# Scores of both maps in couples, with 64-row matmuls for the queries' low halves, in an encoder layer on Trainium2

## The chip, the cores and the metric

The kernel runs on one core of one Trainium2 chip. The metric is the device time of one execution in microseconds (us); of several runs the median is given. A profile is one execution taken by the hardware profiler; its span runs from the first instruction to the last. Engines are named as in the profile: PE is TensorE (PEld its weight loads), DVE is VectorE, ACT is ScalarE, POOL is GpSimd, SP is SyncE, which here issues nearly all DMAs (its queue is SPq). Each engine works through its own queue in order, and waits at an instruction until what it needs has been signalled.

## The reference, cut to what matters

One encoder layer with a convolution branch and a differential-attention branch is applied to two groups of rows, of 2048 and of 1024 positions, with the same weights. The change concerns the attention alone:

```python
def diff_attention(q, k, v, lam):            # 4 heads, head width 64, two maps c per head, values 128 wide
    def block(q_blk):                        # 128 queries
        s = jnp.einsum('bqhcd,bkhcd->bhcqk', q_blk, k).astype(jnp.float32) * scale
        p = jax.nn.softmax(s, axis=-1)
        a = p[:, :, 0] - lam * p[:, :, 1]
        return jnp.einsum('bhqk,bkhe->bqhe', a.astype(v.dtype), v)
```

Everything is float32. Before it come the input projections, the convolution and the rotary embedding; after it a normalisation per head, gates, two output projections and a LayerNorm.

## The kernel before

Matrices are split into a high half (rounded for TensorE) and a low half (the rest), and products are summed from halves, so that TensorE's fast float32 mode gives float32 accuracy.

There are three stages, one behind the other. The first computes all input projections, the convolution and the rotary embedding, and writes queries, keys, values and gates to DRAM, queries and keys each as a high and a low half (`qd`, `kd`). The second is the attention. The third merges the branches and projects.

**Attention.** The work is cut into `pairs`: one head of one group (`h`, `g`) and 256 queries, that is two blocks `j` of 128 queries. There are 32 pairs with 2048 keys (the long group) and then 16 with 1024 keys (the short group). A head's keys lie in tiles `km[c, hf]`, for map `c` and 1024 keys `hf`: the upper 64 rows hold the high half, the lower 64 the low half. A pair's queries lie in four tiles, for each map one with the high half and one with the low half, each twice, above and below (L135 to L143). A product over 128 rows with the high tile so gives high x high + high x low, and one with the low tile low x high + low x low.

The engines' order is written out by a loop that counts steps in `now` (L907). In a step it emits, in this order:

- `score` (L808): for one block, one map and 1024 keys, four matmuls of 512 columns (two column halves, two query halves) into a PSUM tile `s` of two banks, of which there are two. VectorE evicts it (L820) into `e`, scaled and with a running minimum. `e` is a tile of 2048 columns in SBUF; there are `NE` = 8 places, and a new row of scores waits in the loop while they are taken.
- `turn` (L842): four transposes of 128 x 128 on TensorE for two key tiles of a pair that is old enough; ScalarE takes the high half `ah` from PSUM. A long pair has 8 turns, a short one 4. The first stands `LAGS` = 8 steps behind the pair's last score.
- what is due in the middle (`mid`): `soften` (L824), the exponential of one row of `e` on ScalarE with its sum, one step behind the row's last score; the squares of a finished pair.
- `product` (L857): six matmuls with the values, for the turn two steps earlier; then VectorE takes the low half `al` of this step's turn (L852).
- what is due late (`late`): `combine` (L834), two steps behind the score of map 1: VectorE inverts the sum, GpSimd forms the factor `cc`, multiplies map 1's exponentials by it and adds them to map 0's, over the whole row. A pair's turns read that sum for both of its blocks.

Every fourth step also splits a piece of the third stage's weights, while there are any (`resident`, L886): a DMA of 128 KB into one buffer, and four steps later ScalarE's high and GpSimd's low half. When the last long pair is done, `factors` (L746) computes the long group's normalisation factors on VectorE in one go.

SyncE's DMAs are not in the written order; a scheduler places them. In the attention they are a pair's queries (L141, eight of 64 KB), the heads' keys and values, the weight pieces, and small stores. The first pair's queries go through ScalarE's queue at the end of the first stage, in which PSUM is divided among `px` (two buffers), `py`, `pv`, `pz` and others (L163 and L164). The attention's PSUM tiles take over those banks in the order in which the pools are made (L804 to L806).

## Time and profile before

| | us |
|---|---|
| median of 3 runs | 2705.11 (2703.72 to 2706.64) |
| the profiled execution | 2712.73 |
| its span | 2710.9 |

Busy time of each engine in that span, and its instructions, from the head of the profile:

```profile
PE 2592.6 (96%) x12546; PEld 2108.6 (78%) x12546; DVE 2096.7 (77%) x2766; ACT 1195.8 (44%) x1957; POOL 1439.1 (53%) x957
```

and the busy tenths of the same span in 40 equal slices of 67.8 us, where 9 is 90% or more:

```profile
PE   6999899999999999999996999999999999999998
POOL 3577644235431213443545999888889633343343
```

The attention takes the slices in which GpSimd stands at 8 and 9. In answers of the trace a row of the timeline has its start in us, its duration in us, engine, line, operation, what it writes and reads, and in brackets the idle time ahead of it with what ended that. Rows of a group have count, busy time in us, mean ns of one, and the idle time ahead. Rows by stretches of the span have for each engine the busy time and the count, then TensorE's granted clock, the DMA share and GB/s. Matmuls overlap in the pipe, so their durations add up to more than the time between their starts.

### The profile page before, as it was taken

How to read it: one execution, taken by the hardware profiler on the slowest of the kernel's cores; microseconds unless marked ns; L12 is line 12 of the kernel's file. 1: busy time of each engine (PE TensorE's matmuls, PEld its weight loads, DVE VectorE, ACT ScalarE, POOL GpSimd, SP SyncE). 2: the span in 40 equal slices, each digit the busy share in tenths (PEclk: the TensorE clock that was granted, in tenths of full speed). 3: DMA queues.
4: the chain of work that ended last, by engine and by line, in shares of the span. 5: the costliest groups of instructions: out<-in, count | busy, mean ns of one | idle time of the engine just before them, and what ended most of it. 6: DMA issues, size and time to landing. Idle time of an engine off the chain costs nothing. (4 is left out here: it accounts for less than half of the span.)

```text
span 2710.9 us, 37888 instructions
## 1 busy us (share of the span) xinstructions
PE 2592.6 (96%) x12546; PEld 2108.6 (78%) x12546; DVE 2096.7 (77%) x2766; ACT 1195.8 (44%) x1957; POOL 1439.1 (53%) x957
## 2 busy tenths in 40 slices
PE   6999899999999999999996999999999999999998
PEld 3877688787778877778874888888888777777877
DVE  6699888779888358997656888888888776667765
ACT  4323333522232333442435888877789622222221
POOL 3577644235431213443545999888889633343343
PEclk6999999999999999999998999999999999999999
DMA  5578876868986775776976141413153476656553
GB/s 184 198 251 304 273 235 234 300 204 292 316 289 223 244 266 185 244 255 198 300 230 175 57 118 55 108 40 102 40 132 94 156 240 190 195 182 225 171 172 104
DMA packets 339572, 527.15 MB, mean 194 GB/s; under 512 B 42176, under 2 KB 126640, under 8 KB 339376
## 3 DMA queue, kind: packets, MB, share of 16 engines
q1 hardware_dynamic: 338736, 524.20, 59.8%
q8 instruction: 100, 1.64, 0.3%
q14 instruction: 96, 0.79, 0.1%
q10 hardware_dynamic: 640, 0.52, 0.1%
HBM read 344.00 MB, written 167.99 MB: 189 GB/s over the span
## 5 line engine op out<-in xcount | busy, mean ns | idle before, releaser
L229 POOL TENSOR_TENSOR wl<-wq,wh 128x512 fp32r<-128x512 f32 x198 | 267.7, 1355 | 591.5 <-ACT wh L228 511.7
L335 DVE SCALAR_TENSOR_TENSOR acc<-uc,conv_dw,acc 128x1024 f32<-128x1024 f32 (+1 forms) x348 | 444.3, 1277 | 4.1
L818 PE MATMUL s<-km,qq 128*128 128x512 f32 x1280 | 355.2, 400 | 24.9 <-DVE e L820 20.2
L840 POOL TENSOR_TENSOR e<-e 128x2048 f32<-128x2048 f32 (+1 forms) x96 | 373.1, 3886 | 8.0
L831 ACT ACTIVATE e<-e,mx 128x2048 f32<-128x2048 f32 (+1 forms) x192 | 329.3, 1715 | 3.1 <-DVE e L820 3.1
L818 PEld LDWEIGHTS s<-km,qq 128*128 128x128 f32 x1280 | 222.2, 191 | 62.1 <-DVE e L820 26.3
L854 DVE TENSOR_TENSOR al<-tp,ah 128x512 fp32r<-128x512 f32 x320 | 220.3, 689 | 55.7 <-ACT ah L849 55.5
L584 PE MATMUL pv<-xh,wh 128*128 128x512 f32 x528 | 219.0, 415 | 35.5 <-DVE ta L598 25.1
L820 DVE TENSOR_SCALAR_CACHE_REDUCE e<-s 128x1024 f32<-128x1024 f32 x192 | 233.5, 1216 | 16.6 <-PE s L818 15.8
L849 ACT ACTIVATE ah<-tp 128x512 fp32r<-128x512 f32 x320 | 189.4, 593 | 99.3 <-PE tp L847 97.3
L584 PE MATMUL px<-xh,wh 128*128 128x512 f32 x528 | 212.0, 401 | 8.5 <-ACT xh L275 5.3
L584 PE MATMUL pv<-xh,wl 128*128 128x512 f32 x528 | 215.7, 409 | 0.2
L584 PE MATMUL pv<-xl,wh 128*128 128x512 f32 x528 | 215.7, 409 | 0.0
L584 PE MATMUL px<-xh,wl 128*128 128x512 f32 x528 | 211.6, 401 | 4.2 <-POOL wl L229 4.2
L584 PE MATMUL pz<-xh,wh 128*128 128x512 f32 x528 | 211.3, 400 | 3.3 <-ACT xh L275 1.5
L584 PE MATMUL pz<-xh,wl 128*128 128x512 f32 x528 | 211.0, 400 | 0.4 <-DMA wl<-wsd_3l 0.2
L584 PE MATMUL px<-xl,wh 128*128 128x512 f32 x528 | 210.7, 399 | 0.0
L584 PE MATMUL pz<-xl,wh 128*128 128x512 f32 x528 | 210.0, 398 | 0.2 <-DVE xl L276 0.2
L99 PE MATMUL ops<-ah,vv 128*128 128x256 f32 x640 | 207.3, 324 | 0.2 <-ACT row L880 0.2
L94 POOL TENSOR_TENSOR zl<-zraw,zh 128x512 fp32r<-128x512 f32 x88 | 123.5, 1406 | 157.8 <-ACT zh L93 133.0
L847 PE MATMUL tp<-ident,e 128*128 128x128 f32 x1280 | 192.7, 273 | 1.5 <-DVE al L854 1.2
L847 PEld LDWEIGHTS tp<-ident,e 128*128 128x128 f32 x1280 | 158.4, 141 | 45.3 <-DVE al L854 3.7
(228 smaller groups left out, 6334.9 us busy)
## 6 DMA issues: line engine op xcount, KB each, us to landing
wq<-in_w_in SPq DMA_DIRECT2D x220, 256.0 KB
qq<-qd SPq DMA_DIRECT2D x376, 64.0 KB
zraw<-in_w_out SPq DMA_DIRECT2D x88, 256.0 KB
ev<-ev SPq DMA_DIRECT2D x192, 64.0 KB
kd<-ev SPq DMA_DIRECT2D x48, 256.0 KB
qd<-ev SPq DMA_DIRECT2D x48, 256.0 KB
vd<-ev SPq DMA_DIRECT2D x48, 256.0 KB
mcd<-ev SPq DMA_DIRECT2D x48, 256.0 KB
```

The lines of the kernel that those rows point to most:

```text
L94: (lo_engine or nc.vector).tensor_sub(lo, src, hi.bitcast(F32))
L99: nc.tensor.matmul(ps, ah, bh, start=first, stop=False)
L229: (lo_engine or (nc.vector if i in summed and si else nc.gpsimd)).tensor_sub(lo, src, hi.bitcast(F32))
L335: nc.vector.scalar_tensor_tensor(dst, src, dw_sb[:, c, k:k + 1], acc, op0=ALU.mult, op1=ALU.add)
L584: nc.tensor.matmul(ps, w[a][:, k], X[o, k][x], start=fresh and k == a == x == 0, stop=k == 3 and x == 1, skip_group_check=not fresh)
L818: nc.tensor.matmul(s[:, n * 512:(n + 1) * 512], p.qt[2 * c + i][:, j * P:(j + 1) * P], p.km[c, hf][:, n * 512:(n + 1) * 512], start=i == 0 ...
L820: nc.vector.tensor_scalar(p.e[j, c][:, hf * 1024:(hf + 1) * 1024], s, -SCALE, mx[:, hf - 1:hf] if hf else None, op0=ALU.mult, op1=ALU.min, ...
L831: nc.scalar.activation(e, e, AF.Exp, bias=p.mx[j, c][:, nh - 1:nh], scale=-1.0, accum_out=sc)
L840: nc.gpsimd.tensor_add(e0, e0, e)
L847: nc.tensor.transpose(tp[:, i, j * P:(j + 1) * P], p.e[j, 0][:, kt * P:(kt + 1) * P], ident)
L849: nc.scalar.activation(ah, tp, AF.Copy)
L854: nc.vector.tensor_sub(al, tp, ah.bitcast(F32))
```

## The change

- **Couples.** `score` now computes both maps of a block for 1024 keys at once, in every second step (`now % 2`). For each map two matmuls of 128 rows with the high queries come first; then, alternating between the maps, four matmuls of 64 rows multiply the low queries by the high keys alone (low x low is left out). For that, a tile `ql` holds the low queries of map 0 in the upper and of map 1 in the lower 64 rows, and map 1's keys are loaded with the halves exchanged. A pair has five DMAs for its queries instead of eight. Both evictions follow.
- **Times in the loop.** The exponential of map 0 stands one step behind the couple, that of map 1 two, the combination four. `LAGS` is 9, and `OPENING` sets 5 and 7 for the first two pairs. `NE` is 10.
- **First pair.** Its combination is done on VectorE, in two operations, without GpSimd.
- **PSUM.** `pv` and `pz` get a pool of their own, made first, and the attention's pools are made in the order `ops`, `tp`, `s`, so that `s` gets the banks of `py` and of the convolution's tiles.
- **Factors.** For the long group they are computed in four parts, spread over steps.

```diff
 KAPPA = 2.0 ** -11
-LAGS = (8, 8)
-NE = 8
+LAGS = (9, 9)
+OPENING = (5, 7)
+NE = 10
 NST = NH * sum(LENS) // P
...
                 for i in range(2):
-                    nc.sync.dma_start(kk.bitcast(F32)[i * HD:(i + 1) * HD],
+                    o = (i ^ c) * HD
+                    nc.sync.dma_start(kk.bitcast(F32)[o:o + HD],
                                       kd[self.g][self.h][i, c * HD:(c + 1) * HD, hf * 1024:(hf + 1) * 1024])
...
             self.steps, self.lag = self.L // 256, LAGS[g]
+            self.first = g == h == qp == 0
             self.at, self.e, self.mx, self.qt = 10 ** 6, {}, {}, []
             self.col = col0[g][h] + 2 * qp
 
         def load(self, head, maps=(0, 1), queue=nc.sync):
             self.km, self.vv = head.km, head.vv
+            q = slice(self.qp * 256, self.qp * 256 + 256)
             for c in maps:
-                for i in range(2):
-                    qq = kvp[0].tile([P, 256], F32R, name=f"qq{c}{i}", bufs=2)
-                    for r in range(2):
-                        queue.dma_start(qq.bitcast(F32)[r * HD:(r + 1) * HD, :],
-                                          qd[self.g][self.h][i, c * HD:(c + 1) * HD, self.qp * 256:self.qp * 256 + 256])
-                    self.qt.append(qq)
+                qq = kvp[0].tile([P, 256], F32R, name=f"qq{c}", bufs=2)
+                for r in range(2):
+                    queue.dma_start(qq.bitcast(F32)[r * HD:(r + 1) * HD, :], qd[self.g][self.h][0, c * HD:(c + 1) * HD, q])
+                self.qt.append(qq)
+            if maps[-1]:
+                self.ql = kvp[0].tile([P, 256], F32R, name="ql", bufs=2)
+                queue.dma_start(self.ql.bitcast(F32), qd[self.g][self.h][1, :, q])
 
     pairs = [Pair(g, h, qp) for g in range(2) for h in range(NH) for qp in range(LENS[g] // 256)]
+    for p, p.lag in zip(pairs, OPENING):
+        pass
 
...
                       for n, b in (("a_s", 6), ("a_n", 5), ("a_u", 2)))
+
+        psL = pool(name="a_pl", bufs=1, space=PSUM)
         psX = pool(name="a_px", bufs=2, space=PSUM)
...
             px = psX.tile([P, 512], F32, name="px")
-            py, pv, pz = (psP.tile([P, 512], F32, name=n) for n in ("py", "pv", "pz"))
+            py, pv, pz = (x.tile([P, 512], F32, name=n) for x, n in ((psP, "py"), (psL, "pv"), (psL, "pz")))
             t_ = {}
...
         nc.vector.reciprocal(s1, ps[:n, :P])
+        yield
         for _ in range(2):
             nc.vector.scalar_tensor_tensor(s0, s1, 1.0 / KAPPA, s0, op0=ALU.mult, op1=ALU.mult)
         nc.vector.tensor_scalar(f, s0, 1.0 / P, epsl[:n], op0=ALU.mult, op1=ALU.add)
+        yield
         nc.vector.reciprocal(f, f)
+        yield
         nc.vector.tensor_scalar(s0, s0, thr[:n], lscale[:n], op0=ALU.is_le, op1=ALU.mult)
         nc.vector.tensor_mul(s1, s1, s0)
         nc.scalar.activation(f, f, AF.Sqrt)
         nc.vector.tensor_mul(f, f, s1)
         nc.sync.dma_start(rrd[g].rearrange("h (t q) -> (h t) q", q=P), f)
+        yield
 
...
         ep = pool(name="b_e", bufs=NE)
+        psO = pool(name="b_o", bufs=2, space=PSUM)
+        psT = pool(name="b_t", bufs=2, space=PSUM)
         psS = pool(name="b_s", bufs=2, space=PSUM)
-        psT = pool(name="b_t", bufs=2, space=PSUM)
-        psO = pool(name="b_o", bufs=2, space=PSUM)
-
-        def score(p, j, c, hf):
-            if hf == 0:
-                if c == 0 or p.L == 2048:
-                    p.tile = ep.tile([P, 2048], F32, name="e")
-                p.e[j, c] = p.tile[:, c * p.L % 2048:][:, :p.L]
-                p.mx[j, c] = sm.tile([P, 2], F32, name="mx")
-            mx = p.mx[j, c]
-            s = psS.tile([P, 1024], F32, name="s")
-            for n in range(2):
-                for i in range(2):
-                    nc.tensor.matmul(s[:, n * 512:(n + 1) * 512], p.qt[2 * c + i][:, j * P:(j + 1) * P],
-                                     p.km[c, hf][:, n * 512:(n + 1) * 512], start=i == 0, stop=i == 1)
-            nc.vector.tensor_scalar(p.e[j, c][:, hf * 1024:(hf + 1) * 1024], s, -SCALE,
-                                    mx[:, hf - 1:hf] if hf else None, op0=ALU.mult, op1=ALU.min,
-                                    accum_out=mx[:, hf:hf + 1])
+
+        def score(p, j, hf):
+
+
+            q, ns, ss = slice(j * P, (j + 1) * P), [slice(n * 512, (n + 1) * 512) for n in range(2)], []
+            for c in range(2):
+                if hf == 0:
+                    if c == 0 or p.L == 2048:
+                        p.tile = ep.tile([P, 2048], F32, name="e")
+                    p.e[j, c] = p.tile[:, c * p.L % 2048:][:, :p.L]
+                    p.mx[j, c] = sm.tile([P, 2], F32, name="mx")
+                ss.append(psS.tile([P, 1024], F32, name="s"))
+                for n in ns:
+                    nc.tensor.matmul(ss[c][:, n], p.qt[c][:, q], p.km[c, hf][:, n], start=True, stop=False)
+            for n in ns:
+                for c in range(2):
+                    r = slice(c * HD, (c + 1) * HD)
+                    nc.tensor.matmul(ss[c][:, n], p.ql[r, q], p.km[c, hf][r, n], start=False, stop=True)
+            for c in range(2):
+                mx = p.mx[j, c]
+                nc.vector.tensor_scalar(p.e[j, c][:, hf * 1024:(hf + 1) * 1024], ss[c], -SCALE,
+                                        mx[:, hf - 1:hf] if hf else None, op0=ALU.mult, op1=ALU.min,
+                                        accum_out=mx[:, hf:hf + 1])
 
...
             nc.vector.reciprocal(cc, sc)
+            if p.first:
+                nc.vector.scalar_tensor_tensor(cc, cc, neglam, stats[:, p.col + j:p.col + j + 1], op0=ALU.mult, op1=ALU.mult)
+                nc.vector.scalar_tensor_tensor(e0, e, cc, e0, op0=ALU.mult, op1=ALU.add)
+                return
             nc.gpsimd.tensor_mul(cc, cc, stats[:, p.col + j:p.col + j + 1])
...
             if p is pairs[NH * LENS[0] // 256 - 1]:
-                late[now + 4].append(lambda: factors(0, sm, psT.tile([P, 512], F32, name="tp")))
+                def f():
+                    steps = factors(0, sm, psT.tile([P, 512], F32, name="tp"))
+                    next(steps)
+                    for i in range(3):
+                        late[now + 1 + i].append(lambda: next(steps))
+                late[now + 4].append(f)
 
...
         for p in pairs:
-            todo += [(p, j, c, hf) for j in range(2) for c in range(2) for hf in range(p.L // 1024)]
+            todo += [(p, j, hf) for j in range(2) for hf in range(p.L // 1024)]
             ready += [(p, i) for i in range(p.steps)]
...
                     f()
-                if todo and (todo[0][3] or live[0] < NE):
-                    p, j, c, hf = todo.pop(0)
-                    live[0] += hf == 0 and (c == 0 or p.L == 2048)
-                    if (j, c, hf) == (0, 0, 0):
+                if todo and now % 2 and (todo[0][2] or live[0] + todo[0][0].L // 1024 <= NE):
+                    p, j, hf = todo.pop(0)
+                    live[0] += 0 if hf else p.L // 1024
+                    if (j, hf) == (0, 0):
                         nxt = pairs.index(p) + 1
...
                                 x.load(kv[x.g, x.h])
-                    score(p, j, c, hf)
-                    if (j, c, hf) == (1, 1, p.L // 1024 - 1):
-                        p.at = now + p.lag
+                    score(p, j, hf)
                     if hf == p.L // 1024 - 1:
-                        def f(p=p, j=j, c=c, now=now):
-                            sc = soften(p, j, c)
-                            if c == 1:
+                        if j:
+                            p.at = now + p.lag
+
+                        def f(p=p, j=j, now=now):
+                            soften(p, j, 0)
+
+                            def f():
+                                sc = soften(p, j, 1)
+
                                 def f():
                                     combine(p, j, sc)
                                     live[0] -= p.L == 2048
-                                late[now + 2].append(f)
+                                late[now + 4].append(f)
+                            mid[now + 2].append(f)
                         mid[now + 1].append(f)
...
             if R is rows[0]:
-                factors(1, io, psY.tile([P, 512], F32, name="y"))
+                for _ in factors(1, io, psY.tile([P, 512], F32, name="y")):
+                    pass
             steps = {kind: [lambda i=i: next(i)] * (CT + 2) if nxt else [] for kind in "uo"
                      for i in [nxt and prepare(nxt, kind)]}
             both = lambda *fs: lambda: [f() for f in fs]

```

**VectorE, in the long group.** Here `e,mx<-s` is an eviction of the first 1024 keys, `e,mx<-s,mx` that of the second, `al` a turn's low half, and the reciprocal the start of a combination. Before:

```order
L820 TENSOR_SCALAR e,mx<-s 128x1024
L854 TENSOR_TENSOR al<-tp,ah 128x512
L820 TENSOR_SCALAR e,mx<-s,mx 128x1024
L854 TENSOR_TENSOR al<-tp,ah 128x512
L837 RECIPROCAL cc<-ssum 128x1
L820 TENSOR_SCALAR e,mx<-s 128x1024
```

and in the changed kernel:

```order
L840 TENSOR_SCALAR e,mx<-s 128x1024 x2
L878 TENSOR_TENSOR al<-tp,ah 128x512 x2
L840 TENSOR_SCALAR e,mx<-s,mx 128x1024 x2
L878 TENSOR_TENSOR al<-tp,ah 128x512
L857 RECIPROCAL cc<-ssum 128x1
L878 TENSOR_TENSOR al<-tp,ah 128x512
```

The evictions of the two maps now stand together, and the reciprocal stands behind both and a low half; that of a pair's second block is in the step that is five ahead of the pair's first turn, where it was six ahead.

**TensorE, in the long group,** one step before (`s` scores, `tp` a turn, `ops` a product):

```order
L818 MATMUL s<-km,qq_14031 128x512
L818 MATMUL s<-km,qq_14034 128x512
L818 MATMUL s<-km,qq_14031 128x512
L818 MATMUL s<-km,qq_14034 128x512
L847 MATMUL tp<-ident,e 128x128 x4
L99 MATMUL ops<-ah,vv 128x256
L100 MATMUL ops<-ah,vv 128x256
L101 MATMUL ops<-al,vv 128x256
L99 MATMUL ops<-ah,vv 128x256
L100 MATMUL ops<-ah,vv 128x256
L101 MATMUL ops<-al,vv 128x256
```

and an odd step of the changed kernel, with the turn that opens the next:

```order
L833 MATMUL s<-km,qq_13318 128x512 x2
L833 MATMUL s<-km,qq_13321 128x512 x2
L837 MATMUL s<-km,ql 128x512 x4
L871 MATMUL tp<-ident,e 128x128 x4
L100 MATMUL ops<-ah,vv 128x256
L101 MATMUL ops<-ah,vv 128x256
L102 MATMUL ops<-al,vv 128x256
L100 MATMUL ops<-ah,vv 128x256
L101 MATMUL ops<-ah,vv 128x256
L102 MATMUL ops<-al,vv 128x256
L871 MATMUL tp<-ident,e 128x128 x4
```

A step of the first kind has four score matmuls, a turn and a product; in the changed kernel eight score matmuls stand ahead of two turns with their products.

## The prediction

> **What bounds the kernel now.** I read the page's busy shares first, then the busy time by stretches of the span, then the timeline engine by engine, and last the groups by line and shape inside the attention stage. The page gives TensorE 96% of the span, but that is an average over three stages. The change touches the second alone, from about 1420 to 2150 us. Busy time there, by engine (PE, PEld, DVE, ACT, POOL):
>
> ```profile
> 1420.00:1440.00 20.00, 13.67 (x46) 8.58 (x45) 12.91 (x21) 9.19 (x11) 1.30 (x1) 0.91 0.92 256
> 1440.00:1460.00 20.00, 9.88 (x31) 6.24 (x31) 9.55 (x17) 7.18 (x9) 11.47 (x7) 0.79 0.93 255
> 1500.00:1600.00 100.00, 100.00 (x677) 88.83 (x675) 88.66 (x155) 84.00 (x130) 92.52 (x55) 1.00 0.28 77
> 1800.00:1900.00 100.00, 100.00 (x677) 88.92 (x676) 88.66 (x155) 79.64 (x118) 85.50 (x42) 1.00 0.30 83
> 2080.00:2100.00 20.00, 20.00 (x139) 17.78 (x138) 17.34 (x32) 18.80 (x41) 19.15 (x17) 1.00 0.30 80
> ```
>
> There is an opening with idle engines up to 1475, then the long group (32 pairs of query blocks, 2048 keys), where TensorE never idles and VectorE and GpSimd are at 86 to 93%, and then the short group (16 pairs, 1024 keys), where GpSimd is at 96%. So whatever TensorE saves in the long group can be used only until the next engine, or the next chain of waits, is reached. One step of the long group on TensorE:
>
> ```profile
> 1526.73 1.09 PE L818 MATMUL s<-km,qq 128*128 128x512 f32 x4
> 1527.66 0.60 PE L847 MATMUL tp<-ident,e 128*128 128x128 f32 x4
> 1528.02 0.37 PE L99 MATMUL ops<-ah,vv 128*128 128x256 f32 x1
> 1528.22 0.28 PE L100 MATMUL ops<-ah,vv 128*128 128x256 f32 x1
> ...
> 1528.82 1.09 PE L818 MATMUL s<-km,qq 128*128 128x512 f32 x4
> ```
>
> From start to start, four score matmuls take 0.93 us (0.2325 each), a turn (four transposes) 0.36, a product 0.80: 2.09 us a step. A pair is eight steps. Counted in the timeline, the first turn of the fourth pair and that of the last long pair are
>
> ```profile
> 1521.40 0.60 PE L847 MATMUL tp<-ident,e 128*128 128x128 f32 x4
> 1994.60 0.60 PE L847 MATMUL tp<-ident,e 128*128 128x128 f32 x4
> ```
>
> and (1994.60 - 1521.40)/28 = **16.90 us a pair**.
>
> **The couple on TensorE.** It replaces eight matmuls of 128 rows (1.86 us) by four of 128 rows and four of 64. No row shows a 64-row matmul. If the halves of the two maps run side by side, they take 0.465 us, a couple 1.40; one after another it is 1.86 as before. I take 1.40, since the two halves use different rows of the array and different PSUM tiles; the other end is a rival. Each couple also enters and leaves 64-row work. The nearest row for such a passage is the first product after a turn: 0.20 us to its neighbour (1528.02 to 1528.22) where others of its kind are 0.12 apart (0.80 us hold six), so 0.08 to 0.09. For the upper end:
>
> ```profile
> L818 PE MATMUL s<-km,qq 128*128 128x512 f32 x1280 | 355.2, 400 | 24.9 <-DVE e L820 20.2
> ```
> ```profile
> 1423.17 0.50 PE L584 MATMUL pz<-xh,wl 128*128 128x512 f32 x1 [0.16 <-DMA wl<-wsd_3l]
> 1423.51 0.39 PE L584 MATMUL pz<-xl,wh 128*128 128x512 f32 x1
> ```
>
> A matmul of 512 columns lasts 0.40 us against 0.2325 from start to start, so waiting for an empty pipe costs 0.17; one whose weights came late held the next back by 0.34 - 0.23, 0.10 more: 0.27. I take s = 0.09, between 0 and 0.27. TensorE alone would need 4 x (1.40 + 2.32 + 0.18) + 0.23 for the sums = 15.8 us a pair, 1.1 less than now.
>
> The Trainium skill ("TensorEngine Tiling (Array Packing)", Key Properties) says that a change of tiling mode drains TensorE, which speaks against this change. Its page "TensorE: Matmul & The Clock Gate" (Single matmul latency) has (398 + N)/2.4 ns for one warm matmul, 379 ns at N = 512, against 216 back to back; the trace has 400 and 233. An estimate of s from these two pages would be 0.16, and the loop below would come to 17.8 us.
>
> **The chain that takes over.** The change also moves the combination of a map pair. Before, it stood six steps ahead of the pair's first turn, now five, and VectorE meanwhile evicts both maps ahead of the reciprocal. What each link costs, on VectorE and GpSimd:
>
> ```profile
> 1863.10 0.69 DVE L854 TENSOR_TENSOR al<-tp,ah 128x512 fp32r<-128x512 f32 x1
> 1863.78 1.28 DVE L820 TENSOR_SCALAR_CACHE_REDUCE e<-s,mx 128x1024 f32<-128x1024 f32 x1
> 1864.98 0.08 DVE L820 DVE_READ_ACCUMULATOR e<-s,mx 128x1 f32 x1
> 1865.23 0.69 DVE L854 TENSOR_TENSOR al<-tp,ah 128x512 fp32r<-128x512 f32 x1 [0.16 <-ACT ah L849]
> 1865.84 0.15 DVE L837 RECIPROCAL cc<-ssum 128x1 f32<-128x1 f32 x1
> ...
> 1866.13 0.19 POOL L838 TENSOR_TENSOR cc<-cc,stats 128x1 f32<-128x1 f32 x1 [0.15 <-DVE cc L837]
> 1866.43 2.06 POOL L839 TENSOR_SCALAR e<-e,cc,neglam 128x2048 f32<-128x2048 f32 x1
> 1868.58 4.63 POOL L840 TENSOR_TENSOR e<-e 128x2048 f32<-128x2048 f32 x1
> ```
>
> An eviction takes 1.20 us until the next can start, the low half `al` 0.61, and from the reciprocal to the end of GpSimd's addition it is 1873.21 - 1865.84 = 7.37. The addition that releases a turn, and the turn that waited for it in the opening, are
>
> ```profile
> 1458.33 4.55 POOL L840 TENSOR_TENSOR e<-e 128x2048 f32<-128x2048 f32 x1
> ...
> 1463.19 0.60 PE L847 MATMUL tp<-ident,e 128*128 128x128 f32 x4
> ```
>
> 0.31 us from its end. An eviction starts some 0.20 after the turn behind its scores does. So from the end of a couple's scores to the first turn that the combination behind them releases: 0.20 + 2 x 1.20 + 0.61 + 7.37 + 0.31 = **10.9 us**. In that time TensorE has five turns, five products and two couples to do, 5 x 1.16 + 2 x (1.40 + 2s) = 8.6 + 4s, about 9.0. Nothing else can be done meanwhile, since TensorE's queue is in order: the turn blocks the products and the next couple behind it, for about 1.9 us in each pair. (Before, the chain is one eviction shorter, 9.7 us, and has six whole steps, 12.5 us, to lie beside.)
>
> The loop closes over one pair: 10.9, then turn and product 1.16, a couple 1.40, two turns and products 2.32, a couple 1.40: 17.17 + 4s = **17.5 us** a pair with s = 0.09 (17.2 with none, 18.2 with 0.27). ScalarE's two exponentials, now in neighbouring steps, could hold a low half back by up to 0.3; I cost that at nothing, the wait for GpSimd hides most of it. So the long group loses 0.6 us in each of 28 pairs: **+17 us** (+8 to +37). VectorE's own work, two evictions and two low halves, 2 x 1.20 + 2 x 0.61 = 3.6 us a couple, 14.5 a pair, lies below that, and so does GpSimd's:
>
> ```profile
> 1603.85 0.74 POOL L894 TENSOR_TENSOR w_attn_ol<-wraw,w_attn_oh 128x256 fp32r<-128x256 f32 x1
> ...
> 1865.24 0.74 POOL L94 TENSOR_TENSOR sql<-sq,sqh 128x256 fp32r<-128x256 f32 x1
> ```
>
> two combinations of 7.08 (1866.13 to 1873.21), a square's low half and, while they last, two weight pieces, 16.4 at most.
>
> **The opening.** PSUM's new order lets the first scores start before the last projections are evicted. But the first eviction of scores stands on VectorE behind those same evictions and gains nothing there. What holds the opening are ScalarE's pieces of resident weights, which wait for a small transfer and hold the exponentials behind them:
>
> ```profile
> 1448.48 5.37 SPq L141 DMA_DIRECT2D qq<-qd  x8
> ...
> 1453.22 0.42 ACT L893 ACTIVATE w_conv_projh<-wraw 128x256 fp32r<-128x256 f32 x1 [9.95 <-DMA qq<-qd]
> ...
> 1467.04 0.42 ACT L893 ACTIVATE w_conv_projh<-wraw 128x256 fp32r<-128x256 f32 x1 [9.43 <-DMA wraw<-in_w_conv_proj]
> ```
>
> These stand in the changed kernel at the same places. SyncE's issues fall from eight to five a pair, at 5.37/8 = 0.67 us, so these pieces come 2 and up to 4 us sooner. For VectorE's combination of the first pair the nearest row has half its columns:
>
> ```profile
> L1026 DVE SCALAR_TENSOR_TENSOR xr<-xr,mv,ln_g_b 128x1024 f32<-128x1024 f32 x24 | 36.4, 1515 | 0.1
> ```
>
> so it takes about 3 us for GpSimd's 7.4, and the first turn may come at 1457 instead of 1463. Then the second and third pair, with short lags, run into the same 10.9 us chain with nothing to fill it. I put the first turn of the fourth pair at 1524, **+2 us**, between -8 and +8: the gain of some 6 us is spent there. The loads themselves lie under the long group otherwise (DMA share 0.28), as does the space for ten exponentials; both cost nothing.
>
> **The short group.** GpSimd sets its pace, back to back:
>
> ```profile
> 2112.41 0.19 POOL L838 TENSOR_TENSOR cc<-cc,stats 128x1 f32<-128x1 f32 x1
> 2121.02 0.18 POOL L838 TENSOR_TENSOR cc<-cc,stats 128x1 f32<-128x1 f32 x1
> L838 POOL TENSOR_TENSOR cc<-cc,stats 128x1 f32<-128x1 f32 x32 | 6.7, 209 | 9.3 <-DVE cc L837 6.4 <-ACT ah L849 2.9
> ```
>
> 8.6 us a pair, which the couple doesn't touch (TensorE would need 8.0). GpSimd's idle 9.3 us should go: 6.4 where no place for exponentials was free, 2.9 behind the unsplit factors on VectorE. But its first short combination now waits for the last long one, about 3 us. **-6 us**, between -10 and 0. The third stage is not touched.
>
> **Sum.** +2 + 17 - 6 = +13 us on the profiled execution (2712.73 us, span 2710.9; 7.6 above the median of the three runs). Taken to the median: 2705.1 + 13 = 2718 us.
>
> **Rivals.**
> *The gain stays* (not slower). If the result of GpSimd is there when its turn comes, which needs 1.9 us less in the chain or as much more work ahead of the turn, a pair is bound by GpSimd at 16.4 us in the 11 pairs that still carry weight pieces and by TensorE at 15.8 in the other 17: 11 x -0.5 + 17 x -1.1 = -24, with -3 in the opening and -6 in the short group 2672 us. For it speaks that no engine's sum forbids it; against it each link of the chain.
> *The halves do not overlap.* Then a couple is 1.86 + 2s, the loop 17.5 + 0.93 = 18.4: +42, and the short group is bound by TensorE at 8.95 us (+5): 2705 + 2 + 42 + 5 - 6 = 2748 us. The Trainium skill speaks against it ("TensorE: Matmul & The Clock Gate", Part 3): matmuls in different row groups run concurrently. No row here shows it.
> *A wash.* The wait on GpSimd comes, but the passages cost nothing (+8), the opening keeps its 6 us and the short group gives 6 or more: 2705 us, within 4.
>
> **How the numbers follow.** Chances: the forecast 0.47 (2711 to 2740), the gain 0.27, the wash 0.16, the serial halves 0.10. A difference under 0.2%, 5.4 us, cannot be told from no change. Faster 0.27, same 0.16, slower 0.57. The range goes from 2670, past the middle of the gain, to 2746, just short of the serial halves; below and above it I leave about 0.18. The forecast's own range is 2711 to 2740.
>
> **What would show it.** Right: in the long group the first turn of each pair waits for GpSimd's addition 1.5 to 2.5 us, 17.3 to 17.8 us from pair to pair, and TensorE is busy about nine tenths; four 64-row matmuls take about 0.5 us from start to start. Wrong: no wait for GpSimd at the turns and 16 us a pair (the gain), or couples of 1.9 us and more (serial halves). In the short group GpSimd should have no idle stretch of several microseconds.

## The result, and the profile after

The changed kernel takes **2746.69 us** (median of 4 runs, 2742.96 to 2749.87), the kernel before in the same session 2704.41 (4 runs, 2702.43 to 2706.64): a ratio of **1.0153, 95% interval 1.0138 to 1.0167**, 42 us slower. The prediction had the sign and less than a third of the size: 13 us, with a range that ended at 2746, 0.7 us short of the median. The profiled execution of after took 2749.87 us, its span is 2747.7. That of before lay 8.3 us over its median, this one 3.2 over its own, so the spans differ by 36.8 us where the medians differ by 42.3.

Busy time by stretches of after (PE, PEld, DVE, ACT, POOL, then the granted clock), for the same stretches as before:

```profile
1420.00:1440.00 20.00, 12.41 (x34) 5.80 (x32) 9.15 (x16) 6.64 (x7) 0.00 (x0) 0.67 1.04 290
1440.00:1460.00 20.00, 11.21 (x26) 4.89 (x27) 14.68 (x22) 4.67 (x7) 0.73 (x1) 0.50 0.95 223
1500.00:1600.00 100.00, 91.66 (x611) 69.30 (x610) 81.19 (x144) 76.82 (x118) 87.83 (x51) 1.00 0.25 66
1800.00:1900.00 100.00, 94.21 (x647) 73.37 (x645) 83.29 (x148) 77.91 (x116) 81.83 (x39) 1.00 0.23 61
2080.00:2100.00 20.00, 19.16 (x135) 15.07 (x136) 17.04 (x32) 18.43 (x39) 19.06 (x19) 1.00 0.43 114
```

In the long group TensorE now idles for 6 to 8% and issues 611 and 647 matmuls in 100 us where it issued 677; VectorE and GpSimd have become less busy too. That is a chain, not an engine at its limit. The page's groups name where the idle time lies:

```profile
L840 DVE TENSOR_SCALAR_CACHE_REDUCE e<-s 128x1024 f32<-128x1024 f32 x192 | 227.3, 1222 | 52.9 <-PE s L837 52.7
L871 PE MATMUL tp<-ident,e 128*128 128x128 f32 x1280 | 210.6, 284 | 48.0 <-POOL e L864 31.5
```

and the same two groups on the page of before:

```profile
L820 DVE TENSOR_SCALAR_CACHE_REDUCE e<-s 128x1024 f32<-128x1024 f32 x192 | 233.5, 1216 | 16.6 <-PE s L818 15.8
L847 PE MATMUL tp<-ident,e 128*128 128x128 f32 x1280 | 192.7, 273 | 1.5 <-DVE al L854 1.2
```

The turns on TensorE waited 1.5 us in all before, most of it for VectorE; they wait 48.0 now, 31.5 of it for GpSimd's addition.

To see in which stretch the time lies I read marks from TensorE's timeline of each kernel: the end of the first stage's last projection matmul (P), the start of a pair's first turn (its second transposition where that one had to wait for the combination, otherwise its first; T0, T3, T16, T31 for long pairs, numbered from 0, and T47 for the last short one), the start of the last turn and the end of the span. In us; the long group also per pair:

| kernel | P to T0 | T0 to T3 | a pair, T3 to T16 | a pair, T16 to T31 | T31 to T47 | T47 to last turn | last turn to end |
|---|---|---|---|---|---|---|---|
| before | 37.2 | 58.2 | 16.90 | 16.90 | 146.1 | 4.9 | 565.2 |
| **after** | 37.5 | 67.5 | 17.86 | 17.60 | 146.7 | 7.2 | 570.4 |
| e1, lags of ten | 37.2 | 69.6 | 18.23 | 16.84 | 151.4 | 8.9 | 567.9 |
| e4, before with PSUM order | 36.9 | 57.8 | 16.91 | 16.90 | 145.0 | 5.3 | 577.7 |
| e5, e1 and pieces moved | 37.0 | 68.8 | 16.86 | 16.84 | 149.8 | 7.6 | 573.5 |
| e6, halves in one row group | 40.0 | 69.4 | 18.52 | 18.43 | 158.2 | 6.9 | 571.0 |
| e7, PSUM order undone | 37.5 | 67.7 | 17.82 | 17.61 | 146.8 | 7.2 | 560.3 |
| e8, nine for pairs 0 and 1 | 41.8 | 55.7 | 17.89 | 17.61 | 148.0 | 6.0 | 571.2 |
| e9, e5, e7 and e8 together | 41.8 | 56.4 | 16.85 | 16.83 | 150.9 | 8.8 | 562.3 |
| e10, e9 with spread exponentials | 41.5 | 53.5 | 16.40 | 16.40 | 151.8 | 9.0 | 561.5 |
| e12, before with ten places | 37.4 | 57.7 | 16.90 | 16.90 | 143.1 | 4.6 | 563.5 |
| e13, after with spread alone | 38.2 | 65.1 | 17.27 | 17.32 | 146.8 | 7.4 | 578.8 |

After against before: opening +9.6, long group 13 x 0.96 + 15 x 0.70 = +23, short group +0.6, tail +2.3, third stage +5.2; P itself came 3.7 us sooner (1422.3 against 1426.0; it lay at 1420.4 and 1421.5 in e4 and e12, which share that stage with before, so the profiled run of before was late there by chance). The sum is 37, the difference of the spans. The last column also scatters between profiles of kernels that are alike there: over all runs it lies between 560.3 and 565.2 us with the PSUM order of before, and between 567.9 and 578.8 with that of after.

One pair of the long group, TensorE and then the engines it waits for:

```profile
1799.77 1.08 PE L833 MATMUL s<-km,qq 128*128 128x512 f32 x4
1800.78 0.73 PE L837 MATMUL s<-km,ql 64*128 64x512 f32 x4
1801.44 0.65 PE L871 MATMUL tp<-ident,e 128*128 128x128 f32 x4
1801.85 0.36 PE L100 MATMUL ops<-ah,vv 128*128 128x256 f32 x1
...
1809.77 0.66 PE L871 MATMUL tp<-ident,e 128*128 128x128 f32 x4
...
1810.98 0.27 PE L871 MATMUL tp<-ident,e 128*128 128x128 f32 x1
1812.25 0.55 PE L871 MATMUL tp<-ident,e 128*128 128x128 f32 x3 [1.00 <-POOL e L864]
```
```profile
1801.26 0.69 DVE L878 TENSOR_TENSOR al<-tp,ah 128x512 fp32r<-128x512 f32 x1 [0.67 <-ACT ah L873]
1801.87 1.27 DVE L840 TENSOR_SCALAR_CACHE_REDUCE e<-s,mx 128x1024 f32<-128x1024 f32 x1
...
1804.88 0.15 DVE L857 RECIPROCAL cc<-ssum 128x1 f32<-128x1 f32 x1
...
1809.98 0.69 DVE L878 TENSOR_TENSOR al<-tp,ah 128x512 fp32r<-128x512 f32 x1 [1.17 <-ACT ah L873]
```
```profile
1805.18 0.19 POOL L862 TENSOR_TENSOR cc<-cc,stats 128x1 f32<-128x1 f32 x1 [1.90 <-DVE cc L857]
1805.47 2.06 POOL L863 TENSOR_SCALAR e<-e,cc,neglam 128x2048 f32<-128x2048 f32 x1
1807.61 4.59 POOL L864 TENSOR_TENSOR e<-e 128x2048 f32<-128x2048 f32 x1
```

These rows show the chain of the prediction, link by link: the couple's scores end at 1801.44, two evictions and a low half later stands the reciprocal (1804.88), and 7.37 us after that TensorE goes on with the turn (1812.25): 10.81 us, where 10.9 was forecast. The first part is 3.44 us instead of 3.21 and the second 7.37 instead of 7.68, so that two small errors cancel. The turn's first transposition needs only the first query block, which was combined earlier; the other three wait. A couple takes 1.68 us (1799.77 to 1801.44).

### The profile page after: what moved, and what is told of

It is laid out like the page before. It is cut to its first block, busy times and chain, and to the rows that moved or that the text cites. A ratio compares the mean times of both kernels' runs of the same rounds, so it can differ in the third digit from the quotient of the medians.

```text
span 2747.7 us, 37631 instructions
## 1 busy us (share of the span) xinstructions
PE 2592.6 (94%) x12546; PEld 2032.8 (74%) x12546; DVE 2091.8 (76%) x2770; ACT 1199.7 (44%) x1957; POOL 1422.9 (52%) x951
## 5 line engine op out<-in xcount | busy, mean ns | idle before, releaser
L864 POOL TENSOR_TENSOR e<-e 128x2048 f32<-128x2048 f32 (+1 forms) x94 | 362.5, 3856 | 7.8
L840 DVE TENSOR_SCALAR_CACHE_REDUCE e<-s 128x1024 f32<-128x1024 f32 x192 | 227.3, 1222 | 52.9 <-PE s L837 52.7
L871 PE MATMUL tp<-ident,e 128*128 128x128 f32 x1280 | 210.6, 284 | 48.0 <-POOL e L864 31.5
L871 PEld LDWEIGHTS tp<-ident,e 128*128 128x128 f32 x1280 | 141.9, 141 | 115.9 <-issue 39.5
L833 PE MATMUL s<-km,qq 128*128 128x512 f32 x640 | 186.9, 410 | 15.4 <-DVE e L840 10.5
L237 ACT ACTIVATE wh<-wq 128x512 fp32r<-128x512 f32 x198 | 122.9, 622 | 148.4 <-PE pv L593 116.0
```

The source lines that it names most:

```text
L833: nc.tensor.matmul(ss[c][:, n], p.qt[c][:, q], p.km[c, hf][:, n], start=True, stop=False)
L840: nc.vector.tensor_scalar(p.e[j, c][:, hf * 1024:(hf + 1) * 1024], ss[c], -SCALE, mx[:, hf - 1:hf] if hf else None, op0=ALU.mult, op1=ALU.min,
L864: nc.gpsimd.tensor_add(e0, e0, e)
L871: nc.tensor.transpose(tp[:, i, j * P:(j + 1) * P], p.e[j, 0][:, kt * P:(kt + 1) * P], ident)
```

## The experiments

Each ratio is to the kernel before, with its 95% interval; between kernels I use the stretch that was edited.

**e1, lags of ten steps.** From the changed kernel:

```diff
-LAGS = (9, 9)
+LAGS = (10, 10)
```

> The changed kernel with lags of ten steps instead of nine (the opening's two short lags stay). Theory 1 (GpSimd's result comes too late for the pair's first turn): one more step of 1.16 to 1.68 us lies beside the chain, the wait of about 1.0 us at each pair's first turn goes, and a long pair falls from 17.6 to 16.2 to 16.6 us, the four couples of 1.68 us with eight turns and products of 1.16 and the sums of 0.23 being 16.23: 2710 to 2722 us. Theory 2 (the couples themselves are what is slow: entering and leaving 64-row work, and both score buffers taken at once): a long pair stays above 17.3 us, 2742 to 2750 us.

Measured: 2747.23 us, 1.0152 (1.0132 to 1.0172). By the total theory 1 fell. By stretches it holds in the second half of the long group (16.84 us a pair, no wait for GpSimd left), if less than forecast, while the first half, where the weight pieces of `resident` run, got worse: 18.23. From the timeline of all engines there:

```profile
1626.49 0.42 ACT L922 ACTIVATE w_attn_oh<-wraw 128x256 fp32r<-128x256 f32 x1 [0.62 <-DMA wraw<-in_w_attn_o]
...
1632.45 0.73 POOL L923 TENSOR_TENSOR w_attn_ol<-wraw,w_attn_oh 128x256 fp32r<-128x256 f32 x1
...
1633.21 0.34 SPq L920 DMA_DIRECT2D wraw<-in_w_attn_o  x1
...
1636.21 0.42 ACT L922 ACTIVATE w_attn_oh<-wraw 128x256 fp32r<-128x256 f32 x1 [1.17 <-DMA wraw<-in_w_attn_o]
```

A piece's low half stands behind a whole combination on GpSimd (6 us after the piece's high half), only then is the single raw buffer free, the next load is issued and lands 3 us later, and ScalarE waits for it, with the second exponential of a couple, and so the reciprocal and the next combination, behind it: a closed loop, here of 9.72 us from piece to piece (1626.49 to 1636.21), on average of 9.1, two to a pair of 18.23.

**e2, low halves with full rows**, from the changed kernel:

```diff
-nc.tensor.matmul(ss[c][:, n], p.ql[r, q], p.km[c, hf][r, n], start=False, stop=True)
+nc.tensor.matmul(ss[c][:, n], p.ql[:, q], p.km[c, hf][:, n], start=False, stop=True)
```

> The changed kernel with its low halves as matmuls of 128 rows: the tile of low halves, which holds both maps, against the whole key tile. To each score it adds the other map's low query half times the low key half, a product of two small parts. Everything else, the order above all, stays. Theory 1 (64-row halves run in pairs, with a passage of some 0.14 us on each side): the couple grows from 1.68 to 1.86 us; two couples of a pair lie outside the chain, so a long pair goes from 17.6 to about 18.0 and a short one from 8.7 to 9.0: 2758 to 2766 us. Theory 2 (the passages eat what the halves save): 2744 to 2750 us, or faster.

Measured: 2750.40 us, 1.0163 (1.0141 to 1.0184), between the theories. A couple takes 1.84 us, a late pair 17.75 instead of 17.60, a short one in the middle of its group 8.92 instead of 8.69. So 64-row work saves something, but the chain hides most of it.

**e3, the halves in line:** the loops over `n` and `c` around the 64-row matmul exchanged.

> The changed kernel with the four 64-row matmuls of a couple in another order: both of the first map, then both of the second, so that neighbours lie in the same rows of the array. Theory 1 (neighbours in different rows run side by side): this takes that away for at least half of them, the four take 0.9 us instead of 0.5 to 0.66, the couple 1.9 to 2.1 us, a long pair 18.0 to 18.6: 2760 to 2785 us. Theory 2 (they never ran side by side): no change, 2744 to 2750 us.

Measured: 2748.01 us, 1.0155 (1.0136 to 1.0175). The four 64-row matmuls take 0.66 us as before: theory 1 as worded fell. But the edit leaves the two maps in different rows, so it doesn't show that nothing runs side by side; e6 does that better.

**e6, all halves in one row group**, a single execution:

```diff
-r = slice(c * HD, (c + 1) * HD)
+r = slice(0, HD)
```

> The changed kernel with all four 64-row matmuls of a couple in rows 0 to 63: the second map takes the first map's low query half against its own low key half, so that map's scores lack the term of its low query half. Theory 1 (the four take 0.66 us because neighbours in different rows run side by side): now 0.93 us and more from the first of them to the turn. Theory 2 (a matmul of 64 rows is a shorter one by itself): 0.66 us as before. The whole time hardly answers, since the chain through GpSimd covers it: 2745 to 2765 us.

Measured: 2783.77 us.

```profile
1802.53 1.08 PE L833 MATMUL s<-km,qq 128*128 128x512 f32 x4
1803.54 1.19 PE L837 MATMUL s<-km,ql 64*128 64x512 f32 x4
1804.66 0.66 PE L871 MATMUL tp<-ident,e 128*128 128x128 f32 x4
```

The four now take 1.12 us instead of 0.66. The difference of 0.46 is what the prediction had between halves side by side (0.465) and one after another (0.93). So halves in different rows do run side by side, in either order, and the rival of serial halves is out. I was wrong about the total: each couple's 0.46 us shows nearly twice in a pair (18.43 against 17.60), as the prediction's own loop has it.

**e4, the PSUM order alone**, in the kernel before:

```diff
+psO = pool(name="b_o", bufs=2, space=PSUM)
+psT = pool(name="b_t", bufs=2, space=PSUM)
 psS = pool(name="b_s", bufs=2, space=PSUM)
-psT = pool(name="b_t", bufs=2, space=PSUM)
-psO = pool(name="b_o", bufs=2, space=PSUM)
```

> The kernel before with one thing of the change: the PSUM pools of the attention stage opened in the order products, transposes, scores instead of scores, transposes, products. Theory 1 (the third stage's first PSUM buffers then lie on those of products and transposes, and its first matmuls can no longer start among the last turns): from the last pair's first turn to the end of the span 3 to 7 us more than the 570 us of before; nothing gained in the opening, where the first eviction waits on VectorE: 2706 to 2712 us. Theory 2 (the order changes only where the buffers lie): 2700 to 2707 us, 570 us as before.

**e7, the reverse edit in the changed kernel.**

> The changed kernel with the PSUM pools of the attention stage in the order before: scores, transposes, products. Theory 1 (the order costs the third stage its early start): the first matmuls of the third stage stand among the last turns again, 5 to 10 us less from the last turn to the end, nothing lost in the opening: 2737 to 2743 us. Theory 2 (the order pays in the opening what it costs behind): 2745 to 2750 us.

Measured: e4 2715.97 us, 1.0036 (1.0025 to 1.0047), so +10.6; e7 2737.07 us, 1.0113 (1.0094 to 1.0132), so -9.6 against the changed kernel (-10.8 by the ratios, since the two were timed in different sessions). The third stage's first PSUM pool lies where the attention stage's first pool lay. With scores first, these banks are free when the last scores are evicted, and the scheduler puts matmuls of the third stage into TensorE's gaps among the last turns; with products and transposes first they come behind everything. The last turn and the third stage's first matmul, before and after:

```profile
2134.87 0.50 PE L99 MATMUL y<-uh,w_conv_projh 128*128 128x512 f32 x1 [0.72 <-ACT uh L93]
...
2145.68 0.66 PE L847 MATMUL tp<-ident,e 128*128 128x128 f32 x4
```
```profile
2177.31 0.92 PE L871 MATMUL tp<-ident,e 128*128 128x128 f32 x4 [2.92 <-DVE al L878]
...
2186.92 0.63 PE L100 MATMUL y<-uh,w_conv_projh 128*128 128x512 f32 x1
```

10.8 us ahead of the last turn before, 9.6 behind it after; 12.0 behind in e4, 16.2 ahead in e7. From P to T0 the order changes nothing (37.2 and 36.9, 37.5 and 37.5).

**e5, lags of ten and the weight pieces in other steps**, from the changed kernel:

```diff
-LAGS = (9, 9)
+LAGS = (10, 10)
...
-if now % 4 == 0:
+if now % 4 == 2:
     next(pieces, None)
```

> The changed kernel with lags of ten steps, and the weight pieces taken in other steps: where the step's number is 2 modulo 4 instead of 0, so between two couples' exponentials instead of between the two exponentials of one couple. Theory 1 (with a lag of ten the first half of the long group is paced by a loop: GpSimd's combination, behind it the piece's low half, which frees the one raw buffer, the load, ScalarE's piece, which holds the second exponential, the reciprocal, the combination): the pairs with pieces fall from 18.2 to 16.8 to 17.2 us, as the later ones have, 13 pairs save 13 to 18 us: 2728 to 2736 us. Theory 2 (it is the lag or the couples that make the first half slow): 18.0 us and more there, 2744 to 2750 us.

Measured: 2733.51 us, 1.0100 (1.0080 to 1.0119). All long pairs now take 16.85 us; theory 1. In the rows from 1525 to 1740 us ScalarE's pieces wait 23.3 us for their loads in e1 and not at all here. Since e5 differs from e1 in the pieces' steps alone, it shows that their place is the cause; that the loop closes through the raw buffer is read from the rows of e1.

**e8, nine steps for the first two pairs** (`OPENING = (9, 9)` for `(5, 7)`), from the changed kernel:

> The changed kernel with a lag of nine steps for the first two pairs too, instead of five and seven. Theory 1 (short lags only move the wait: the pairs' first turns stand on TensorE's queue and hold the couples behind them, and TensorE's clock falls while it waits): the first turn comes later, but the fourth pair starts within 3 us of where it does now, or sooner: 2742 to 2750 us. Theory 2 (short lags shorten the opening): six steps without turns more, 8 to 15 us lost: 2755 to 2762 us.

Measured: 2743.68 us, 1.0137 (1.0119 to 1.0156). The first turn comes 4.3 us later, the fourth pair's 7.5 sooner (P to T3 97.5 us, before 95.4, after 105.0). So the short lags cost the opening more than they gave it: 7.5 of the 9.6 us that it lost. The clock, which theory 1 also names, was 0.50 from 1430 to 1460 us with and without them, so that this run doesn't show its part.

**e9, the edits of e5, e7 and e8 together.**

> The changed kernel with four edits of the runs so far together: lags of ten, weight pieces in the steps 2 modulo 4, the PSUM order before, and nine steps for the first two pairs. Theory 1 (each acts in a stretch of its own): 13.2, 9.6 and 3.0 us come off 2746.7, 2716 to 2724 us; a long pair 16.85 us, 97 to 99 us from the last projection to the fourth pair's first turn. Theory 2 (one of them only moved a wait that another also moves): 2726 us or more. By both it is slower than before: the long pair is as long as before, and the opening, the short group and the tail are still some 10 us longer.

Measured: 2710.95 us, 1.0023 (1.0013 to 1.0033): 5 us better than theory 1's range, but still slower than before. Theory 1 took 3.0 us for the short lags, from the total of e8; their stretch gains 7.6 here (P to T3 105.8 in e5, 98.2 here), as it gained 7.5 in e8.

**e10, e9 with the exponentials of a long couple spread:**

```diff
-if now % 4 == 2:
+if now % 4 == 3:
...
-mid[now + 2].append(f)
+mid[now + 1 + p.L // 1024].append(f)
```

> As the run with the four edits, but with the second map's exponential of a long couple two steps after the first's instead of one (so one in each even step), and the weight pieces in the steps 3 modulo 4, where no exponential stands. Theory 1 (two neighbouring exponentials hold ScalarE's copies of the turns, these VectorE's low halves and evictions, and these TensorE's next couple, 0.6 us a pair): a long pair 16.25 to 16.6 us, 7 to 17 us less than that run. Theory 2 (TensorE waits for VectorE whatever ScalarE's order): 16.8 us and more, within 4 us of it.

Measured: **2698.42 us, 0.9972 (0.9962 to 0.9982)**, the first version that beats both kernels. Busy time of e9 and of e10:

```profile
1800.00:1900.00 100.00, 99.91 (x676) 76.42 (x675) 86.94 (x155) 81.22 (x120) 85.71 (x42) 1.00 0.28 75
```
```profile
1800.00:1900.00 100.00, 100.00 (x698) 79.59 (x697) 89.65 (x160) 85.31 (x124) 88.26 (x44) 1.00 0.28 75
```

698 matmuls in 100 us where there were 676, and 16.40 us a pair where there were 16.83 to 16.85, which the busy share (99.9% and 100%) doesn't show. The run moves the weight pieces too, but the later pairs, which have none, gain 0.43 us as well, so that this part is the exponentials'.

**e13, spread exponentials alone**, in the changed kernel with its lags of nine:

> The changed kernel with one edit: the second map's exponential of a long couple two steps after the first's instead of one. The lags stay at nine, the weight pieces at their steps. Theory 1 (the chain through GpSimd holds by itself; the reciprocal stands where it stood): the later pairs stay at 17.3 to 17.6 us, 2738 to 2747 us. Theory 2 (the chain is late because ScalarE's neighbouring exponentials hold back VectorE's low half and with it the evictions and the reciprocal, 1.17 us in the trace): the later pairs fall to 16.4 to 16.9 us, 2715 to 2735 us.

Measured: 2739.09 us, 1.0105 (1.0087 to 1.0124), with 17.32 us a late pair: theory 1. The two neighbouring exponentials cost a late pair only 0.3 us; the waits of 0.67 and 1.17 us for `ah` in the rows above are their marks. The earlier pairs fall further, from 17.86 to 17.27. TensorE still waits for GpSimd (from 1700 to 1900 us 10.5 us in all, in 11 waits of at most 1.0):

```profile
PEld tp L871 <- POOL e L864: 10.5, 11, 1.0
```

**e11, full rows on top of e9.**

> As the run with the four edits, but with the low halves as matmuls of 128 rows, as in the earlier run with full rows. There the chain through GpSimd hid most of the difference; here TensorE is nearer the bound. Theory 1 (64-row work saves TensorE 0.12 us a couple, 1.80 to 1.85 against 1.68 and 0.05 more behind it): a long pair 17.2 to 17.4 us and a short one 8.5 to 8.9: 13 to 20 us more than that run. Theory 2 (TensorE's waits for VectorE take up the difference): within 5 us.

Measured: 2716.51 us, 1.0037 (1.0022 to 1.0051), 17.08 us a pair against 16.84. The 64-row form is worth 0.24 us a pair there, less than I expected; the intervals of e9 and e11 overlap, so the totals hardly tell them apart.

**e12, ten places in the kernel before** (`NE = 10` for 8):

> The kernel before with ten places for exponentials instead of eight, nothing else. Theory 1 (GpSimd's idle 6.4 us in the short group, where no place was free, goes): 4 to 7 us less between the last long pair and the end of the short group, 2698 to 2702 us. Theory 2 (the scores that come sooner are held by something else): 2703 to 2707 us.

Measured: 2705.21 us, 1.0005 (0.9995 to 1.0015), no difference in the total; in the profile the stretch from T31 to T47 is 3.0 us shorter (e4, without this edit, has 1.1 less than before). GpSimd's waits there fell from 9.3 us (the row in the prediction) to 6.0:

```profile
L838 POOL TENSOR_TENSOR cc<-cc,stats 128x1 f32<-128x1 f32 x31 | 6.4, 207 | 6.0 <-ACT ah L849 3.4 <-DVE cc L837 2.7
```

**e14, e10 with the first pair combined on GpSimd** (`self.first = False`):

> As the run with spread exponentials, but with the first pair combined on GpSimd like all others. Theory 1 (with a lag of nine the first pair's combination on VectorE shortens the opening): from the last projection to the first turn 45 to 49 us instead of 41.5, the time 3 to 7 us longer than that run's. Theory 2 (with nine steps of lag the first turn doesn't wait for the combination): within 2 us of it.

Measured: 2700.63 us, 0.9968 (0.9949 to 0.9987), within 2.2 us of e10. P to T0 grows from 41.5 to 45.2 us, so VectorE's combination does bring the first turn 3.7 us sooner; the total doesn't show it.

## Why the prediction was wrong, step by step

The chain through GpSimd was forecast and is there. What failed are terms of the sum: the opening (+2, measured +9.6), the short group (-6, measured +0.6) and the third stage, which was put at nothing (+5.2 between these two profiles, some 10 by e4 and e7); the long group was mis-sized (+17, measured +23).

- **TensorE's step and the pair of before**: right; 16.90 us again in e4 and e12.
- **The couple**: the mechanism was right, the passages were too cheap. 1.40 + 2s came out at 1.68, and the first product behind the turn comes 0.41 us after it instead of 0.36: 0.33 us a couple for both passages, s = 0.17, within the bounds but twice the 0.09 that I took. Where it falls: the full matmuls take 1.02 from start to start instead of 0.93, the halves 0.66 instead of 0.465. The Trainium skill ("TensorEngine Tiling (Array Packing)", Key Properties) says that a change of tiling mode drains TensorE; the 0.33 us fit that, and the estimate of 0.16 from its pages, which I gave and set aside, was the better one. e6 shows that halves in different rows run side by side: 0.66 against 1.12 us. The Trainium skill ("TensorE: Matmul & The Clock Gate", Part 3) says so of matmuls in different row groups, and the traces agree.
- **The chain**: right in place, and in length (10.81 us for 10.9) with the help of the two errors that cancel. TensorE had 9.5 us beside it, 0.5 more than forecast, from the passages and the sums, so the wait was 1.0 to 1.3 us and not 1.9; the pair gained nothing by that, since it is the chain that closes the loop.
- **The long group, +17**: mis-sized, +23. The later pairs took 17.60 for 17.5. The earlier took 17.86: the loop through the raw buffer (e1, e5) was not seen. It lay in the profile of before already: `L893` waiting for `wraw`, which I read for the opening alone. With lags of nine ScalarE's pieces wait 9.9 us for their loads between 1525 and 1740 us; no run moved the pieces alone there, so that the whole 0.26 us a pair is theirs is not shown.
- **"ScalarE's two exponentials ... I cost that at nothing, the wait for GpSimd hides most of it"**: nearly right for the later pairs while the wait is there (0.3 us in e13), but they cost 0.43 us a pair once it is gone (e9 to e10).
- **The opening, +2**: failed, +9.6. From the first turn to that of the fourth pair the forecast was right (1457 to 1524, so 67 us; measured 67.5). The step that failed is the gain at the first turn, which I had 6 us sooner and so 31 us after P; it came 37.5 us after P. The stalls for the weight pieces did go (9.95 and 9.43 us before, 1.67 and none now) and VectorE's combination took the 3 us forecast, but what was late next was the couple itself. It takes both score buffers and releases both at its end, so VectorE's evictions follow it instead of lying beside it, and TensorE, at a granted clock of 0.50 there, is slow:

```profile
1436.11 2.42 PE L833 MATMUL s<-km,qq 128*128 128x512 f32 x4 [1.38 <-DVE e L840]
1438.47 1.22 PE L837 MATMUL s<-km,ql 64*128 64x512 f32 x4
1441.01 2.37 PE L833 MATMUL s<-km,qq 128*128 128x512 f32 x4 [1.32 <-DVE e L840]
```

  A couple every 4.9 us, where before a map's scores came every 1.3 us and so a couple's worth every 2.6:

```profile
1436.03 2.36 PE L818 MATMUL s<-km,qq 128*128 128x512 f32 x8 [0.22 <-DVE e L820]
1438.62 2.34 PE L818 MATMUL s<-km,qq 128*128 128x512 f32 x8 [0.23 <-DVE e L820]
```

  Of the 4.9 us the couple's matmuls take 3.6, where at a clock of 1.00 they take 1.68, and the wait for the evictions 1.3. In the same stretch, from 1435 to 1445 us, the clock of before was 1.00. This is read from the rows; no run separates the couple from the clock. So the first turn, though it stands five steps behind the scores instead of eight, came no sooner after P than before (37.5 and 37.2). In both pairs with short lags the turn waits some 5 us, in the first for VectorE's combination and in the second for GpSimd's:

```profile
1454.43 0.47 PE L871 MATMUL tp<-ident,e 128*128 128x128 f32 x1
1459.80 0.90 PE L871 MATMUL tp<-ident,e 128*128 128x128 f32 x3 [4.90 <-DVE e L860]
...
1486.77 0.90 PE L871 MATMUL tp<-ident,e 128*128 128x128 f32 x3 [5.27 <-POOL e L864]
```

- **The short group, -6**: failed, +0.6, and +2.3 in the tail. The late first short combination came as forecast: it starts 0.1 us ahead of T31, where it started 3.2 ahead before. What failed is that GpSimd's idle 9.3 us should go: 6.8 are left from T31 to T47, and 2.5 less idle against 3 us later is the +0.6. The places give some 3 us in e12. But in the changed kernel GpSimd waits elsewhere, for reciprocals that stand behind a couple's evictions or behind the split factors:

```profile
2049.76 0.19 POOL L862 TENSOR_TENSOR cc<-cc,stats 128x1 f32<-128x1 f32 x1 [1.46 <-DVE cc L857]
...
2076.36 0.19 POOL L862 TENSOR_TENSOR cc<-cc,stats 128x1 f32<-128x1 f32 x1 [3.00 <-DVE cc L857]
```

  The 2.9 us behind the factors are still there, as 3.0: the pieces on VectorE, with a couple's evictions between them, delay a reciprocal as the single piece did. My sign that GpSimd would have no idle stretch of several microseconds failed with it. I read this from the trace only; no run edited the factors.
- **"The third stage is not touched"**: a step that missed a mechanism. The PSUM order is part of the change; I followed it to the opening and not to the stage behind. It is worth 9.6 to 10.6 us (e7, e4).
- **The rivals**: the gain stays didn't come, and for the reason named: the chain. With 16.40 us a pair in e10 it exists, and TensorE's own sum with the passages as measured, 4 x (1.68 + 0.05 + 2.32) + 0.23 = 16.4, says that this is its end, not the 15.8 of the prediction. The serial halves gave the nearest time, 2748, which is luck: e6 shows that their mechanism isn't there. The wash needed passages that cost nothing and a gain in the opening and the short group; none of the three came.

What stays open: how much of the tail's 2.3 us belongs to the late combination and how much to the third stage's work on VectorE; and what share of the slow couples in the opening is the clock's.

From T31 to T47 lags of ten cost 3 to 5 us more than lags of nine. The traces show where: GpSimd's waits for reciprocals there come to 11.0 to 12.9 us (e1, e5, e9, e10, e14) against 6.6 to 6.8 (after, e7, e8, e13). With lags of ten some of the factors' operations on VectorE (L764, L770) stand beside GpSimd's additions and end just behind these, as in e14:

```profile
2032.23 2.37 POOL L864 TENSOR_TENSOR e<-e 128x1024 f32<-128x1024 f32 x1
2032.26 2.49 DVE L770 TENSOR_TENSOR rs<-rs,ssq 64x128 f32<-64x128 f32 x1
```

In the changed kernel, where no addition runs beside it, the same operation takes 0.28 us.

## What to carry to other kernels

A longer lag or a cheaper matmul pays only when every loop that closes over the same steps has slack: here three were stacked (GpSimd's combination, the single raw buffer of the weight pieces, ScalarE's neighbouring exponentials), and removing the first alone changed the total by nothing. When pools are reordered, look at what the next stage places on the same banks, since its start may have been filling the gaps of this stage's end. A form that takes both halves of a double buffer at once gives up the overlap that the double buffer was there for; in the opening here, where no other work fills the gap, the rows suggest that this shows, but no run tests it alone.

## What the runs showed of the hardware

Four 64-row matmuls of 512 columns, two in the upper and two in the lower rows, took 0.66 us in either order, whether neighbours in the queue lie in different rows (after) or the same (e3), and 1.12 us when all lie in the same rows (e6). Four full ones take 0.93, so that 64 rows by themselves save nothing: 1.12 is 0.93 and 0.66 is half of that, 0.465, each with some 0.19 us on top. Passages into and out of such work cost about 0.33 us a couple in all, in either order. A VectorE operation on two small tiles that took 0.28 us alone took 2.49 beside an addition on GpSimd (after and e14). And a busy share of 99.9% on TensorE left room for 3% more matmuls (e9 and e10), so its count of matmuls in a stretch says more than its share.
